# Seven-product attention gates, raw queries and keys beside the attention, and the attention's output projection beside the mLSTM heads

## The chip, the cores and the metric

The kernel runs on one core of a Trainium2 chip. The metric is the device time of one execution in microseconds (us). Before the change three executions took 2128.82, 2127.21 and 2130.36 us; their median is 2128.82 us. A further execution, run under the hardware profiler, took 2130.97 us, of which the program's own span, from its first to its last instruction, is 2129.0 us.

Engines are called by the names in the profile: PE is the matrix engine, PEld its loading of stationary operands, DVE, ACT and POOL the vector, scalar and general engines, SP the queue that issues most transfers.

## The reference, cut to what matters

One layer, 512 tokens, width 2048, everything in float32.

```python
h = rms_norm(x, norm_g)
proj = h @ w_in                       # split into the thirteen parts below
(q_a, k_a, v_a, o_a, i_a, f_a, z_a, c_q, c_kv, k_r, z_b, g_a, g_b) = split(proj)

qk_a = silu(causal_depthwise_conv(concat(q_a, k_a), conv_w))       # four taps
h_a = mlstm_chunkwise(q_a, k_a, v_a, i_a + bias, f_a + bias)       # 8 heads, 128 / 256 wide
h_a = rms_norm(h_a, mlstm_norm_g)
y_a = (sigmoid(o_a) * h_a * silu(z_a)) @ w_a

q_b = rms_norm(rms_norm(c_q) @ w_uq); k_b, v_b = from rms_norm(c_kv) @ w_ukv and k_r, with rope
o_b = causal_attention(q_b, k_b, v_b)                               # 16 heads
y_b = (o_b * silu(z_b)) @ w_b

out = x + (sigmoid(g_a) * y_a + sigmoid(g_b) * y_b) @ w_out
```

## The kernel before, in words

**Arithmetic.** PE multiplies float32 values that are split in two parts: `split` lets ACT copy the value to a rounded high part (line 105) and DVE subtract it to get the low part (line 106). `mm3` (lines 114 to 116) then issues three products, high by high, high by low, low by high. A product of 512 columns is the normal one: a 128x128 stationary block and 512 moving columns.

**Plain projections.** `proj_tok` produces rows of tokens: the stationary operand is a block of 128 tokens, the weights move. `proj_ch` produces rows of channels: the weights are stationary, 512 tokens move. Both are generators: after each 128 rows of the weights they yield the number of columns that they gave PE (6144 for a `proj_tok` of width 512, 4608 at width 384, 3072 for a `proj_ch` of two channel blocks). `load_w` fetches the weights through three small rings: raw, high and low.

**Stages, in program order.**

1. The latent projections and the normalisation of the input (0 to about 123 us).
2. `strassen`: five parts of the input projection (o_a, z_a, g_a, g_b, v_a), in ten jobs of 1024 columns. Each job makes a 2x2 block product with seven products instead of eight. A job has 28 steps of 12 products of 512 columns; the stationary operand is a combination of the token blocks, the combined weights move. `finish` hands the results to `tanh_out`, `silu_out` or `split_out`, which write them to DRAM.
3. Attention in eight pairs of heads. `pair_proj(p)` projects queries, keys and values of pair p from the latents; `pair_attn(p)` makes transposes, scores, softmax, transposed probabilities and values, in ten named steps, and stores the gated result to `gb_d[p]`. `pair_gate(p)` is the z_b gate of a pair: a plain `proj_ch` from the normalised input, 16 yields of 3072 columns (96 products), with a tanh and one DVE operation at the end; its result stays in the on-chip tile `gz`.
4. Queries and keys of the mLSTM: `block_qk(n)`, eight blocks of two heads each (queries and keys by turns), each a plain `proj_ch` of 96 products, with the convolution, the silu and the split after it on DVE and ACT (`conv_qk`). They read the normalised input, as the gates do.
5. Eight mLSTM heads. `head_load` fetches v, o and z; `head_mlstm` runs four steps of scores and four of values; `head_scale` and `head_out` finish a head, one head later, and store it to `ga_d[h]`.
6. `out_b(d)`: the attention's output projection with w_b, four column blocks of 16 yields of 6144 columns (12 products each). Its stationary operand comes from `gb_d` by way of `reload`, which fetches six blocks ahead into the pool `gp`.
7. The mLSTM's output projection with w_a, from `ga_d`, reloaded in the same way into the pool `g2p`, and the final projection with w_out (lines 1247 to 1276).

**What sets the order.** `weave(main, filler)` interleaves two generators: each number that the main one yields is a wish for filler columns, and the filler is advanced until at least that many have come; nothing is carried over to the next wish. The wishes are `KEYS_AHEAD` = 8000 once and `ATTN_STEP` = 7800 ten times for a pair, `MLSTM_STEP` = 6000 for each of a head's eight steps and `OUT_AHEAD` = 10000 four times after the last head. Under this, the framework's planner takes the program order as each engine's priority and moves later instructions up when earlier ones are not ready and their buffers are free.

Before the change the fillers are: in pairs 0 to 5 one gate and the next pair's projection each, in pair 6 the last projection, in pair 7 nothing; then blocks 0 to 2 run alone; block h+3 runs beside head h for h = 0 to 4; `out_b(0)` and `out_b(1)` run beside heads 5 to 7; `out_b(2)` and `out_b(3)` run alone after the heads.

**Memory.** Pools are opened and closed in program order, and a pool opened later may lie where a closed one was. The normalised input lies in `h8p` and `htp`; `gp` is opened where they were. The attention's tiles lie in `bpa` and `bpb`; the mLSTM's `bph` (17 slots) is opened there. `g2p` is opened where `bph` was. Short-lived tiles share the six slots of `tmp`. PSUM has five `acc` banks, used by projections, and three `aux` banks.

Of the kernel before, what the change touches and what calls it, by code (L numbers as in the profile page):

```python
# [19 lines left out]
P = 128  # L20
S = 512
# [18 lines left out]
KEYS_AHEAD, ATTN_STEP, MLSTM_STEP, OUT_AHEAD, G_AHEAD, CONV_WAIT = 8000, 7800, 6000, 10000, 6, 8  # L40
# [4 lines left out]
def hybrid_kernel(  # L45
# [396 lines left out]

    def split_out(dst):
        def done(t, src, inner):
            hi, lo = tmp(512, "oh", F32R), tmp(512, "ol", F32R)
            split(hi, lo, src)
            A.dma_start(dst[0][:, t, :], f32(hi))
            A.dma_start(dst[1][:, t, :], f32(lo))
        return done

    def strassen(jobs, comb):
# [45 lines left out]
        def mult(c, p, j):  # L497
# [52 lines left out]
        for src, col, outs in jobs:  # L550
            c = dict(src=src, col=col, outs=outs, x={}, ring={}, ps={})
            steps += [(c, p, j) for p in range(7) for j in range(H8 // 2)]
# [29 lines left out]
    jobs = []  # L582
    for off, dst, kind in ((OFF_OA, o_d, tanh_out), (OFF_ZA, z_d, silu_out), (OFF_GA, ga_g, tanh_out),
                           (OFF_GB, gb_g, tanh_out), (OFF_VA, v_d, split_out)):
        for i in range(2):
            jobs.append((w_in, off + 1024 * i, [kind(dst[2 * i]), kind(dst[2 * i + 1])]))
# [174 lines left out]
    def pair_proj(p, c):  # L761
        qn = big([P, T, 2, DN], F32, "qn")
# [144 lines left out]
    def pair_attn(p, c):  # L907
# [8 lines left out]
        for step in ("S00 S01", "X00 S02", "X01 S03", "X02 S10", "X03 S11", "O0 X10 S12", "X11 S13", "X12", "X13", "O1"):  # L916
            for w in step.split():
# [3 lines left out]
                elif w[0] == "X":  # L921
                    probs_t(c, u, int(w[2]))
                else:
                    drain(gates[p] or ())
                    values(p, c, u)
# [66 lines left out]

    cs = [dict() for _ in range(8)]
    first = pair_gate(0, cs[0])
    weave(chain(*lats), first)
    drain(first)
    drain(pair_proj(0, cs[0]))
    second = pair_gate(1, cs[1])
    weave(mlstm_gates(), second)
    drain(second)  # L1000
    gates = [None, None] + [pair_gate(p, cs[p]) for p in range(2, 8)]
# [10 lines left out]
    def conv_qk(p, base, blk, res, wait):  # L1012

        def evac(s, ps):
            k = blk + 2 * p + s
            xp = tmp(516, "xp")
            G.memset(xp[:, 0:3], 0.0)
            A.copy(xp[:, 3:515], ps)
            o = big([P, 2, S], F32R, "qkT")
            b = []  # L1020

            def taps(j0, j1):
                for j in range(j0, j1):
                    V.scalar_tensor_tensor(b[0], xp[:, j:j + S], cw[:, k, j:j + 1], b[0], ALU.mult, ALU.add)

            def first():
                b.extend((tmp(512, "cv"), tmp(512, "th")))
                with behind_weights():
                    V.tensor_scalar(b[0], xp[:, 3:515], cw[:, k, 3:4], None, ALU.mult)
                    taps(0, 1)  # L1030

            def second():
                taps(1, 3)
                A.activation(b[1], b[0], AF.Tanh, scale=0.5)

            def third():
                V.scalar_tensor_tensor(b[0], b[1], 1.0, b[0], ALU.add, ALU.mult)
                A.copy(o[:, 0, :], b[0])

            def fourth():  # L1040
                V.tensor_tensor(o[:, 1, :], b[0], f32(o[:, 0, :]), ALU.subtract)

            if s == 0:
                later.extend([lambda: None] * wait)
            later.extend((first, second, third, fourth))
            res.append(o)

        yield from proj_ch(load_h(base + p * 256), 2, get_n, KD, evac)
# [95 lines left out]
    def block_qk(n, wait=CONV_WAIT):  # L1144

        p, res = n // 2, []
        yield from conv_qk(p, *((OFF_KA, 8) if n % 2 else (OFF_QA, 0)), res, wait)
        for u in range(2):
            hs[2 * p + u]["kT" if n % 2 else "qT"] = res[u]
# [6 lines left out]
    def reload(src, pool, dst):  # L1156
        g = []

        def fetch():
            p, n = divmod(len(g), 2)  # L1160
            g.append(pool.tile([P, 2, S], F32R, tag="g", name=nm("g"), bufs=16))
            SP.dma_start(f32(g[-1][:, 1, :]), src[p][:, n, :])

        for _ in range(G_AHEAD):
            fetch()
        yield
        for k in range(KD):
            if len(g) < KD:
                fetch()
            split(g[k][:, 0, :], g[k][:, 1, :], f32(g[k][:, 1, :]))  # L1170
            dst.append((g[k][:, 0, :], g[k][:, 1, :]))
            yield

    def lazily(g, rest):
        def get(k):
            while k + 1 >= len(g) and len(g) < KD:
                next(rest)
            return g[k]
        return get

    u_t = []

    def out_b(d):
        u = up.tile([P, T, 512], F32, tag=f"u{d}", name=f"u{d}")
        SP.dma_start(u, gb_g[d])
        u_t.append(u)

        def evac(t, ps):
            V.scalar_tensor_tensor(u[:, t, :], u[:, t, :], 1.0, ps, ALU.add, ALU.mult)

        yield from proj_tok(load_w(w_b, d * 512, 512, KD), 512, get_gb, KD, evac)

    def heads():
        for h in range(H_A):
            ahead = head_load(h + 1, hs[h + 1]) if h + 1 < H_A else iter(())
            for n, want in enumerate(head_mlstm(h, hs[h])):
                next(ahead, None)
# [4 lines left out]
                yield want  # L1202
            drain(ahead)
            yield None
# [7 lines left out]
    filler = block_qk(3)  # L1212
    done = 0
    for want in heads():
        if want is not None:
            weave([want], filler)
            continue
        done += 1
        if done < 5:
            drain(filler)  # L1220
            filler = block_qk(done + 3, CONV_WAIT if done < 4 else 0)
        elif done == 5:
            drain(filler)
            close_pool("htp")
            close_pool("h8p")
            gp = open_pool("gp", "right")
            up = open_pool("up", "right")
            gB = []
            rest = reload(gb_d, gp, gB)
            next(rest)  # L1230
            get_gb = lazily(gB, rest)
            filler = chain(out_b(0), out_b(1))
    drain(filler)
# [85 lines left out]
```

## Time and profile before

| what | value |
|---|---|
| median of three executions | 2128.82 us |
| the profiled execution | 2130.97 us |
| its span | 2129.0 us |
| PE busy | 2100.9 us (99%), 10200 products |
| DVE, ACT, POOL busy | 1397.0 us (66%), 982.9 us (46%), 173.6 us (8%) |
| granted PE clock over the span | 0.999 |
| data moved | 292.31 MB, mean 137 GB/s |
| issues of 256 KB of w_in by `load_w` | 128, median 2.8 us to landing |
| issues of 512 KB of w_in by `strassen` | 160 (40 in `rx`, 120 in `rr`), 5.1 and 4.7 us to landing |

How to read it: "busy" of PE is the time in which at least one product is under way. Products are pipelined and overlap, so a product's own duration is longer than the time until the next one starts. A group of instructions is written as line, engine, operation, output <- inputs, form, count, then busy time and mean duration in ns. "SPq" and "ACTq" are the instruction queues that issue transfers.

### The profile page before, as it was taken

How to read it: one execution, taken by the hardware profiler on the slowest of the kernel's cores; microseconds unless marked ns; L12 is line 12 of the kernel's file. 1: busy time of each engine (PE TensorE's matmuls, PEld its weight loads, DVE VectorE, ACT ScalarE, POOL GpSimd, SP SyncE). 2: the span in 40 equal slices, each digit the busy share in tenths (PEclk: the TensorE clock that was granted, in tenths of full speed). 3: DMA queues.
4: the chain of work that ended last, by engine and by line, in shares of the span. 5: the costliest groups of instructions: out<-in, count | busy, mean ns of one | idle time of the engine just before them, and what ended most of it. 6: DMA issues, size and time to landing. Idle time of an engine off the chain costs nothing.

```text
span 2129.0 us, 28895 instructions
## 1 busy us (share of the span) xinstructions
PE 2100.9 (99%) x10200; PEld 1780.4 (84%) x10200; DVE 1397.0 (66%) x2260; ACT 982.9 (46%) x2025; POOL 173.6 (8%) x306
## 2 busy tenths in 40 slices
PE   8899999999999999999999999999999999999999
PEld 8888888888888888888888888788878788888889
DVE  6888878786786788746766666867785433443323
ACT  8544455444444444445555555545564322222221
POOL 0000010000000000022222222101111000000000
PEclk9999999999999999999999999999999999999999
DMA  6656437624633643832222222365564542332443
GB/s 163 167 184 188 142 108 236 207 91 129 197 102 102 192 148 101 263 88 79 80 80 81 82 77 75 123 199 162 164 209 134 183 138 96 121 123 91 138 130 118
DMA packets 208769, 292.31 MB, mean 137 GB/s; under 512 B 31600, under 2 KB 111856, under 8 KB 207600
## 3 DMA queue, kind: packets, MB, share of 16 engines
q1 hardware_dynamic: 192496, 263.20, 40.3%
q10 hardware_dynamic: 16128, 27.27, 3.6%
q8 instruction: 80, 1.31, 0.3%
q14 instruction: 65, 0.53, 0.1%
HBM read 244.27 MB, written 46.14 MB: 136 GB/s over the span
## 4 chain that ended last, share of the span: by engine, by line
PE 93%; DMA 2%; ACT 2%; DVE 1%; issue 1%; POOL 0%; SPq 0%; ACTq 0%; DVEq 0%; POOLq 0%
PE acc L115 16%; PE acc L116 16%; PE acc L114 16%; PE acc L518 8%; PE acc L519 8%; PE acc L517 8%; PE aux L519 4%; PE aux L518 4%; PE aux L517 4%; PE aux L114 2%; PE aux L116 2%; PE aux L115 2%; ACT junk L248 1%; PE aux L883 1%; PE aux L843 1%
## 5 line engine op out<-in xcount | busy, mean ns | idle before, releaser
L106 DVE TENSOR_TENSOR wlo<-raw,whi 128x512 fp32r<-128x512 f32 (+3 forms) x432 | 285.2, 663 | 390.5 <-PE acc L115 286.5
L105 ACT CAST whi<-raw 128x512 fp32r<-128x512 f32 (+3 forms) x432 | 259.1, 601 | 527.0 <-PE acc L116 356.5
L106 DVE TENSOR_TENSOR wl<-rx,wh 128x1024 fp32r<-128x1024 f32 x160 | 195.8, 1224 | 106.8 <-PE aux L518 57.3
L105 ACT CAST wh<-rx 128x1024 fp32r<-128x1024 f32 x160 | 168.8, 1055 | 172.8 <-PE acc L519 96.2
L115 PE MATMUL acc<-wlo,g 128*128 128x512 f32 x512 | 200.9, 392 | 3.6 <-DVE wlo L106 3.5
L114 PE MATMUL acc<-whi,g 128*128 128x512 f32 x512 | 200.1, 394 | 3.1 <-ACT whi L105 2.0
L105 ACT CAST wh<-rr 128x1024 fp32r<-128x1024 f32 x120 | 126.4, 1054 | 163.7 <-PE aux L519 91.7
L116 PE MATMUL acc<-whi,g 128*128 128x512 f32 x512 | 200.4, 392 | 1.1 <-DVE g L106 1.1
L106 DVE TENSOR_TENSOR wl<-rr,wh 128x1024 fp32r<-128x1024 f32 x120 | 146.3, 1219 | 25.3 <-PE aux L518 13.9
L518 PE MATMUL acc<-wl,sh 128*128 128x512 f32 x400 | 155.6, 389 | 0.0
L519 PE MATMUL acc<-wh,sl 128*128 128x512 f32 x400 | 155.6, 389 | 0.0
L517 PE MATMUL acc<-wh,sh 128*128 128x512 f32 x400 | 155.4, 389 | 0.0
L115 PEld LDWEIGHTS acc<-wlo,g 128*128 128x128 f32 x512 | 96.7, 189 | 25.1 <-DVE wlo L106 6.1
L116 PEld LDWEIGHTS acc<-whi,g 128*128 128x128 f32 x512 | 96.5, 189 | 21.7 <-DVE g L106 1.5
L114 PEld LDWEIGHTS acc<-whi,g 128*128 128x128 f32 x512 | 95.9, 188 | 22.3 <-ACT whi L105 2.2
L114 PE MATMUL acc<-whi,y 128*128 128x512 f32 (+1 forms) x320 | 111.1, 348 | 0.0
L116 PE MATMUL acc<-whi,y 128*128 128x512 f32 (+1 forms) x320 | 111.0, 347 | 0.0
L115 PE MATMUL acc<-wlo,y 128*128 128x512 f32 (+1 forms) x320 | 111.0, 347 | 0.0
L114 PE MATMUL acc<-h8h,whi 128*128 128x512 f32 x256 | 101.7, 397 | 0.0
L114 PE MATMUL acc<-ht,whi 128*128 128x512 f32 x256 | 101.6, 397 | 0.0
L116 PE MATMUL acc<-h8h,wlo 128*128 128x512 f32 x256 | 100.2, 391 | 0.1
L115 PE MATMUL acc<-h8l,whi 128*128 128x512 f32 x256 | 100.1, 391 | 0.0
(357 smaller groups left out, 5036.0 us busy)
## 6 DMA issues: line engine op xcount, KB each, us to landing
rr<-in_w_in SPq DMA_DIRECT2D x120, 512.0 KB, 4.7
raw<-in_w_in SPq DMA_DIRECT2D x128, 256.0 KB, 2.8
rx<-in_w_in SPq DMA_DIRECT2D x40, 512.0 KB, 5.1
raw<-in_w_b SPq DMA_DIRECT2D x64, 256.0 KB, 3.2
raw<-in_w_a SPq DMA_DIRECT2D x64, 256.0 KB, 3.0
raw<-in_w_out SPq DMA_DIRECT2D x64, 256.0 KB, 3.0
raw<-in_w_ukv SPq DMA_DIRECT2D x32, 256.0 KB, 2.9
raw<-in_w_uq SPq DMA_DIRECT2D x32, 192.0 KB, 2.4
```

The source lines that it names most:

```text
L105: hi = A.copy(dst_hi, src)
L106: lo = V.tensor_tensor(dst_lo, src, f32(dst_hi), ALU.subtract)
L114: PE.matmul(ps, lh, rh, start=start, stop=False)
L115: PE.matmul(ps, lh, rl, start=False, stop=False)
L116: PE.matmul(ps, ll, rh, start=False, stop=stop)
L248: A.activation(junk[:, :P], xr[:, t, :], AF.Square, accum_out=ssx[:, k, t:t + 1])
L517: PE.matmul(out[i], lh[:, tok], hi[:, n, :], start=first, stop=False, skip_group_check=cont)
L518: PE.matmul(out[i], lh[:, tok], lo[:, n, :], start=False, stop=False, skip_group_check=cont)
L519: PE.matmul(out[i], ll[:, tok], hi[:, n, :], start=False, stop=k == H8 - 1, skip_group_check=cont)
L843: PE.transpose(ps[:, t * P:(t + 1) * P], src(t), ident)
L883: PE.transpose(ps[:, j * P:(j + 1) * P], pr[:, j * P:(j + 1) * P], ident)
```

## The change

Four things are changed.

1. The z_b gate leaves the attention stage. It becomes two more jobs of `strassen`, ahead of v_a's. These jobs have a mark `ch`: the weights' combinations are stationary in blocks of 128 channels, and the combinations of the token blocks move, 256 columns at a time, so that a step has 24 products of 256 columns and the result stands in rows of channels. Two blocks of channels share one PSUM bank. `silu_out_ch` writes the gate to DRAM (`gz_d`), and `pair_proj` loads it into the tile `gz`. `pair_gate` is gone.
2. `block_qk(0)` to `(7)` take the gates' places: block 0 beside the latents' transposes, block 1 beside `mlstm_gates`, and blocks 2 to 7 as fillers of pairs 0 to 6, in the order "rest of a begun block, next pair's projection, further blocks". They store the raw queries and keys to DRAM (`qk_d`).
3. The convolution moves to the heads: `head_conv(h)` loads the raw rows of one head and runs the same operations one head ahead, in the same four parts, with the tanh written over the raw rows.
4. `out_b` becomes the only filler from pair 7 on: seven of its yields in pair 7, one with each of the six parts of `head_load(0)`, and the rest beside the heads. `gp` is opened, and the reload begun, before pair 7. `MLSTM_STEP` becomes 4500 and `OUT_AHEAD` 8000; `CONV_WAIT` is gone.

```diff
-KEYS_AHEAD, ATTN_STEP, MLSTM_STEP, OUT_AHEAD, G_AHEAD, CONV_WAIT = 8000, 7800, 6000, 10000, 6, 8
+KEYS_AHEAD, ATTN_STEP, MLSTM_STEP, OUT_AHEAD, G_AHEAD = 8000, 7800, 4500, 8000, 6
...
+    def silu_out_ch(dst):
+        def done(t, src, inner):
+            o = tmp(512, "ot")
+            A.activation(o, src, AF.Tanh, scale=0.5)
+            V.scalar_tensor_tensor(o, o, 1.0, src, ALU.add, ALU.mult)
+            n = (t // 2) * 256
+            A.dma_start(dst[t % 2][:, :, n:n + 256], o.rearrange("p (s c) -> p s c", s=2))
...
-                for i in range(2):
+                for i in range(4 if c["ch"] else 0):
+                    o, ch = out[i // 2][:, (i % 2) * 256:(i % 2 + 1) * 256], slice(i * P, (i + 1) * P)
+                    first = k == 0 and p not in (3, 5) and i % 2 == 0
+                    PE.matmul(o, hi[:, n, ch], lh, start=first, stop=False, skip_group_check=True)
+                    PE.matmul(o, hi[:, n, ch], ll, start=False, stop=False, skip_group_check=True)
+                    PE.matmul(o, lo[:, n, ch], lh, start=False, stop=k == H8 - 1, skip_group_check=True)
+                for i in range(0 if c["ch"] else 2):
...
     def pair_proj(p, c):
+        c["gz"] = big([P, 2, S], F32, "gz")
+        SP.dma_start(c["gz"], gz_d[p])
...
-    def pair_gate(p, c):
-        gz = c["gz"] = big([P, 2, S], F32, "gz")
+    def block_qk(n):
+        p, odd = divmod(n, 2)
         def evac(s, ps):
-            th = tmp(512, "th")
-            A.activation(th, ps, AF.Tanh, scale=0.5)
-            V.scalar_tensor_tensor(gz[:, s, :], th, 1.0, ps, ALU.add, ALU.mult)
-        yield from proj_ch(load_h(OFF_ZB + p * 256), 2, get_n, KD, evac)
+            x = tmp(512, "xq")
+            A.copy(x, ps)
+            A.dma_start(qk_d[2 * p + s][:, odd, :], x)
+        yield from proj_ch(load_h((OFF_KA if odd else OFF_QA) + p * 256), 2, get_n, KD, evac)
...
-    for p in range(8):
-        proj = pair_proj(p + 1, cs[p + 1]) if p < 7 else iter(())
-        weave(pair_attn(p, cs[p]), chain(gates[p] or (), proj, *gates[max(2, p + 1):p + 3]))
-        drain(proj)
+    for p in range(7):
+        proj = pair_proj(p + 1, cs[p + 1])
+        first = chain(ahead(True), proj)
+        weave(pair_attn(p, cs[p]), chain(first, ahead()))
+        drain(first)
         cs[p] = None
+    drain(ahead())
+    close_pool("htp")
+    close_pool("h8p")
+    gp = open_pool("gp", "right")
+    gB = []
+    rest = reload(gb_d, gp, gB)
+    next(rest)
+    get_gb = lazily(gB, rest)
+    filler = chain(*(out_b(d) for d in range(4)))
+    weave(pair_attn(7, cs[7]), islice(filler, 7))
...
+    def head_conv(h, c):
+        xs, parts = [], []
+        for n in range(2):
+            xp = tmp(516, "xp")
+            G.memset(xp[:, 0:3], 0.0)
+            SP.dma_start(xp[:, 3:515], qk_d[h][:, n, :])
+            xs.append(xp)
...
+        q, k = conv(0), conv(1)
+        for turn in ((), (), (), (q,), (q, k), (q, k), (q, k), (k,)):
+            for part in turn:
+                next(part)
+            yield
...
-    for n in range(3):
-        drain(block_qk(n, 0))
-    drain(head_load(0, hs[0]))
...
-    filler = block_qk(3)
...
-    drain(filler)
+    start = head_conv(0, hs[0])
+    for load in head_load(0, hs[0]):
+        next(start)
+        next(filler)
+    drain(start)
+    weave(heads(), filler)
     close_pool("bph")
     g2p = open_pool("g2p")
-    for d in range(2, 4):
-        drain(out_b(d))
+    drain(filler)
```

More of the change, by code (lines that the diff above doesn't have):

```diff
@@ L991, in mlstm_gates, with reload, fetch @@
                 V.tensor_tensor(ab[:, j, i, :], ab[:, j, i - 1, :], gs[:, i - 1, :], ALU.add)
+    def reload(src, pool, dst):
+        g = []
+        def fetch():
+            p, n = divmod(len(g), 2)
+            g.append(pool.tile([P, 2, S], F32R, tag="g", name=nm("g"), bufs=16))
+            SP.dma_start(f32(g[-1][:, 1, :]), src[p][:, n, :])
+        for _ in range(G_AHEAD):
+            fetch()
+        yield
+        for k in range(KD):
+            if len(g) < KD:
+                fetch()
+            split(g[k][:, 0, :], g[k][:, 1, :], f32(g[k][:, 1, :]))
+            dst.append((g[k][:, 0, :], g[k][:, 1, :]))
+            yield
@@ new lines, in lazily, with get, out_b, evac @@
+    def lazily(g, rest):
+        def get(k):
+            while k + 1 >= len(g) and len(g) < KD:
+                next(rest)
+            return g[k]
+        return get
+    u_t = []
+    def out_b(d):
+        def evac(t, ps):
+            u = u_t[d]
+            V.scalar_tensor_tensor(u[:, t, :], u[:, t, :], 1.0, ps, ALU.add, ALU.mult)
+        for k, want in enumerate(proj_tok(load_w(w_b, d * 512, 512, KD), 512, get_gb, KD, evac)):
+            if k == H8:
+                u_t.append(pools["up"][1].tile([P, T, 512], F32, tag=f"u{d}", name=f"u{d}"))
+                SP.dma_start(u_t[d], gb_g[d])
+            yield want
@@ L993, in hybrid_kernel @@
     cs = [dict() for _ in range(8)]
[L994 to L996 removed]
+    blocks = [block_qk(n) for n in range(8)]
+    weave(chain(*lats), blocks[0])
+    drain(blocks[0])
     drain(pair_proj(0, cs[0]))
[L998 to L1001, printed above, removed]
[L1002 to L1006 removed]
+    weave(mlstm_gates(), blocks[1])
@@ new lines, in hybrid_kernel, with ahead @@
+    drain(blocks[1])
+    del blocks[:2]
+    begun = []
+    def ahead(only_begun=False):
+        while blocks and (begun or not only_begun):
+            begun[:] = [True]
+            for want in blocks[0]:
+                yield want
+            del blocks[0], begun[:]
+    for p in range(7):
[3 more added lines that the diff above has]
+        drain(first)
+        cs[p] = None
+    drain(ahead())
@@ L1019, in evac @@
             o = big([P, 2, S], F32R, "qkT")
-            b = []
+            c["kT" if n else "qT"] = o
+            b = tmp(512, "cv")
             def taps(j0, j1):
                 for j in range(j0, j1):
[L1024 to L1045, printed above, removed]
@@ L1142, in head_out @@
         hs[h] = None
[L1144 to L1149, printed above, removed]
-    hs = [dict() for _ in range(H_A)]
-    for n in range(3):
-        drain(block_qk(n, 0))
-    drain(head_load(0, hs[0]))
[L1156 to L1191, printed above, removed]
+    hs = [dict() for _ in range(H_A)]
     def heads():
         for h in range(H_A):
-            ahead = head_load(h + 1, hs[h + 1]) if h + 1 < H_A else iter(())
+            conv = ahead = iter(())
+            if h + 1 < H_A:
+                conv, ahead = head_conv(h + 1, hs[h + 1]), head_load(h + 1, hs[h + 1])
             for n, want in enumerate(head_mlstm(h, hs[h])):
+                next(conv, None)
                 next(ahead, None)
```

62 lines of the change are left out of this document (29 added, 33 removed).

## The prediction

> **What bounds the kernel now.** I read the page's head, its slices and its chain first, then products by form and their starting times, then counts in windows.
>
> ```profile
> span 2129.0 us, 28895 instructions
> PE 2100.9 (99%) x10200; PEld 1780.4 (84%) x10200; DVE 1397.0 (66%) x2260; ACT 982.9 (46%) x2025; POOL 173.6 (8%) x306
> PEclk9999999999999999999999999999999999999999
> DMA  6656437624633643832222222365564542332443
> PE 93%; DMA 2%; ACT 2%; DVE 1%; issue 1%; POOL 0%; SPq 0%; ACTq 0%; DVEq 0%; POOLq 0%
> ```
>
> PE is busy for 99% of the span at the full granted clock, and 93% of the chain that ended last is PE. So the time is the number of products times their spacing, plus the stretches in which PE lacks work. The durations of products (about 390 and 280 ns) overlap; the spacing comes from starting times:
>
> ```profile
> 2079.11 0.28 PE L114 MATMUL acc<-whi,y 128*128 128x256 f32 x1
> ...
> 2125.06 0.28 PE L116 MATMUL acc<-whi,y 128*128 128x256 f32 x1
> L517 PE MATMUL acc<-wh,a x160: 388/389/397, 123.1 to 819.7; 128*128 128x512 f32 x160
> ...
> L519 PE MATMUL aux<-wh,h8l x160: 389/389/398, 189.8 to 885.4; 128*128 128x512 f32 x160
> ```
>
> The first pair of rows are the first and last of 384 products of 256 columns: 45.95 / 383 = 120.0 ns. The second pair bound the 3360 products of the seven-product stage: 762.3 / 3359 = 226.9 ns for 512 columns, with no pause. Half the columns thus cost 53% of the time. Where PE lacks work is seen by counting products on acc, then on aux:
>
> ```profile
> 1550.00:1600.00 50.00, 35.76 (x140) 0.97 0.65 218
> 1675.00:1725.00 50.00, 46.49 (x201) 1.00 0.70 232
> ...
> 1550.00:1600.00 50.00, 13.42 (x87) 0.97 0.65 218
> 1675.00:1725.00 50.00, 0.11 (x1) 1.00 0.70 232
> ```
>
> From 1550 to 1600 there are 140 products of 226.9 ns (31.8 us) and 87 of mostly 120 ns (10.4, with the longer score products about 11): some 7 us are lost, where the input's pool is exchanged for w_b's operand. From 1675 to 1725, 201 products are 45.6 us: 4.4 are lost, where the reload for w_a competes with w_b's weights.
>
> **Part a, the gates' products.** Removed: 8 gates x 96 = 768 products of 512 columns, 768 x 226.9 = 174.3 us. Added: 2 jobs x 28 steps x 24 = 1344 products of 256 columns, x 120.0 = 161.3 us. Net -13.0 us, all on the path. By eighths alone it would be 672 x 226.9 = 152.5 us; the narrow form gives 8.8 us of that back. The bounds are -13.0 and -21.8; I take -13.0, since the rows of 256 columns above are the same form on acc.
>
> The Trainium skill ("TensorE: Matmul & The Clock Gate", section "Back-to-back issue gap") gives a gap of N / 2.4 + 2.5 ns, 215.8 and 109.2 ns here; by it the sum would be 768 x 215.8 - 1344 x 109.2 = -19 us. The trace has 226.9 and 120.0, about 11 ns more for every product whatever its width, and the measurement decides.
>
> The steps' other work hides below products: 56 casts and subtractions of 1024 columns and 32 subtractions lie in a stage whose 3360 products above ran without a pause. The 16 stores of the gate, their 8 loads on SP, the 16 stores of raw rows on ACT's queue and 16 loads of them on SP are transfers of 256 to 512 KB in stages where the transfer engines are mostly 2 to 6 tenths busy (the DMA slices above). I cost them at nothing; without that cover, 24 loads of some 3 to 5 us stand in SP's order before w_in's and w_b's weights. The tanh, silu and convolution operations are the same in number.
>
> **Part b, the pool exchange.** The exchange at 1550 moves before pair 7, and the blocks that read the input are used up earlier still: a pair now wishes for three yields of a block ten times, less the projection's, about 21 a pair, so 96 yields end in pair 4. The reload then starts under attention products: the 7 us go. Late next: the start of the heads, where within six yields (16 us) come the loads of v, o, z (2 MB), raw rows, w_b's weights and w_b's operand splits. At the 218 GB/s of the row at 1550 the roughly 4.5 MB take 20 us. I give back 2: -5, between -7 and 0.
>
> **Part c, the last pairs.**
>
> ```profile
> 1239.87:1296.74 56.87, 56.83 (x303) 49.30 (x301) 38.93 (x95) 31.32 (x94) 14.87 (x18) 1.00 0.27 79
> 1296.74:1341.86 45.12, 42.30 (x237) 36.27 (x235) 33.60 (x87) 26.91 (x86) 14.38 (x18) 1.00 0.26 77
> ```
>
> The windows are pair 5, with gate and projection, and pair 6, with the projection and the first 30 products of block 0 that the planner moved up (303 - 237 = 66 fewer, of 96). Pair 6 should last 56.87 - 66 x 0.227 = 41.9 us and lasts 45.1: a pair without a block loses 3.2 us, as the softmax's chain on DVE and ACT shows through. Now the blocks are spent in pair 4, so pair 5 joins pair 6 in that state: products for 56.9 - 21.8 = 35.1 us under a chain that took 45.1. Pair 5 loses between 0 (if the next projection moves up) and 10; I take +5. Pair 7 gets seven yields (19 us) in place of block 0's: no change.
>
> **Part d, the end of the heads.** This decides the sign. out_b has 4 x 16 = 64 yields. Seven go to pair 7, six to `head_load(0)`. A wish of 4500 takes a whole yield of 6144, as 6000 did, so each of a head's eight steps takes one: 51 yields last through heads 0 to 5 and three steps of head 6. Thirteen steps, and all four wishes of `OUT_AHEAD`, find no filler. Before, out_b(2) and out_b(3) covered the close with 87 us of products.
>
> ```profile
> 1469.00:1497.60 28.60, 28.60 (x149) 24.51 (x148) 21.69 (x43) 16.65 (x42) 4.19 (x15) 1.00 0.54 166
> 1616.07:1644.67 28.60, 28.60 (x149) 24.50 (x148) 14.85 (x34) 13.60 (x36) 3.93 (x10) 1.00 0.27 93
> ```
>
> These are a head with a block and its convolutions, and a head with out_b. A head takes 28.6 us, of which the filler is 96 x 0.2269 = 21.8 and its own products 6.8. Own DVE work is 14.85 less eight splits of 0.69 (the row of L106 below) = 9.3, and the next head's convolution adds 21.69 - 14.85 = 6.8. For thirteen steps (1.6 heads): DVE 15.1, with the last convolution 21.9; PE 11. PE idles at least 4 us, at most 11 plus some 6 of latency; I take 7.
>
> After the last value product comes a chain with nothing beside it:
>
> ```profile
> 1649.46 0.28 PE L116 MATMUL aux<-vh,stb 128*128 128x258 f32 x1
> 1650.19 0.17 DVE L1116 SCALAR_TENSOR_TENSOR den<-num 128x4 f32<-128x4 f32 x1 [1.34 <-ACT num L1112]
> 1653.95 0.20 POOL L1125 TENSOR_TENSOR rsn<-rsn,den 128x4 f32<-128x4 f32 x1
> 1658.39 1.67 DVE L1132 SCALAR_TENSOR_TENSOR og<-num,rsn,og 128x256 f32<-128x256 f32 x4
> 1674.07 1.03 PE L1138 MATMUL aux<-ident,og 128*128 128x128 f32 x8
> 1676.45 0.47 SPq L1254 DMA_DIRECT2D gate<-gga  x1
> 1681.53 1.37 SPq L1162 DMA_DIRECT2D g<-ga  x3
> DMA to landing us min/median/max: 4.0/5.2/7.8
> 1686.41 1.29 ACT L105 CAST g<-g 128x512 fp32r<-128x512 f32 x2 [2.46 <-DMA g<-ga]
> 1687.06 0.69 DVE L106 TENSOR_TENSOR g<-g 128x512 fp32r<-128x512 f32 x1 [3.22 <-ACT g L105]
> ```
>
> From that product to the scale factors 1654.15 - 1649.46 = 4.7; scaling 1.7; transposes to the gate's load 1676.45 - 1674.07 = 2.4; its issue 0.5; the first block of w_a's operand 5.2 to land (the landing row is that of the reload's line); its split 0.62 + 0.69 = 1.3. Sum 15.8, less a microsecond of transposes: 14.8 us of empty PE. It cannot be shortened by earlier loads if a pool waits for the whole of the one before it, as here:
>
> ```profile
> L116 PE MATMUL acc<-h8h,wlo x256: 387/389/499, 886.5 to 1543.8; 128*128 128x512 f32 x128
> L116 PE MATMUL acc<-ht,wlo x256: 388/389/400, 900.7 to 1559.3; 128*128 128x512 f32 x128
> L1162 SPq DMA_DIRECT2D g<-gb x16: 319/430/611, 1556.8 to 1579.9; - x16
> L1162 SPq DMA_DIRECT2D g<-ga x16: 379/430/2725, 1681.5 to 1703.6; - x16
> ```
>
> Half of the input's tiles were last read at 1543.8, yet the first load into their place is issued at 1556.8, when the other half is almost done; and w_a's operand, most of it stored long before, is not fetched until head 7's transposes have run. Part d: +7 + 14.8 - 4.4 (the loss at 1675, gone) = +17.4, between 8 (4 + 8 for a chain with the operand already on its way) and 28.
>
> **Sum.** -13.0 - 5 + 5 + 17.4 = +4.4 us. The span becomes 2133.4, the profiled execution 2130.97 + 4.4 = 2135.4. That execution stands 2.15 us above the median of 2128.82, so I predict a median of 2133.2 us, 0.2% slower; 0.2% (4.3 us) is about what a measurement of this kernel tells from no change.
>
> **Rivals.** First, faster, by one mechanism: the end is covered. If `g2p` takes bph's slots one by one, head 0's to 5's rows (12 of 16 blocks) can be fetched and up to 12 x 2.72 = 32.6 us of w_a's products run during heads 6 and 7. It decides from the point at which the first load of `ga` is issued before head 7's last transposes. Then d is about 3 - 4.4, and the sum -13 - 5 + 5 - 1.4 = -14: 2114. For it: most of the 17 slots are idle by then. Against: the last four rows. Chance 0.15.
>
> Second, the cheap ends together with the same empty end: no loss in pair 5 and thirteen steps at DVE's pace: -13 - 7 + 0 + 14.4 = -6: 2123. For it: the planner moved 30 products up in pair 6. Chance 0.2.
>
> Third, the dear ends: pair 5 loses 10, the heads start 5 us late, and the thirteen steps run at the chain's latency: -13 + 0 + 10 + 24 = +21: 2150. For it: six slots of `tmp` now also hold raw rows until they are stored, and each convolution holds four. Chance 0.2. The empty end may also cost clock: the row at 1550 shows 0.97 granted where gaps stood, 1.5 us in 50. The Trainium skill, on the page named above (Part 1, "The HAM clock gate"), says the clock halves after an idle window of about 3.4 us and recovers after as long a busy one, which by it would add 1.7 us; no gap here is long enough to show it.
>
> My own case has 0.45, from 2128 to 2140. Of it 0.22 lie above +4.3 us and 0.23 within; of the second rival 0.13 is faster. Together: faster 0.28, same 0.30, slower 0.42. The range of 2116 to 2148 leaves out most of the first rival and the dearest end.
>
> **What would show it.** Part a: 1344 products of 256 columns with starts 120 ns apart, from some 735 to 895. Part b: no stretch of seven lost us at the reload of `gb`, its first load before pair 7. Part c: pair 5 short of products, with waits for `pr`. Part d: the last `out_b` product some 20 us before head 7's last values, then about 15 us of empty PE before the first product of w_a. I am wrong if w_a's products start before head 7's transposes, or if out_b still runs then.

## The result, and the profile after

The changed kernel takes 2156.54 us (median; 2155.99 to 2158.16), the kernel before 2128.39 in the same comparison: a ratio of 1.0133, 95% interval 1.0115 to 1.0150. It is 28 us slower, where 4 were forecast. The profiled execution has a span of 2154.3 us, 25.3 more than before.

The head and two slice rows of the page of the changed kernel:

```profile
span 2154.3 us, 30176 instructions
PE 2101.4 (98%) x10776; PEld 1803.1 (84%) x10776; DVE 1461.9 (68%) x2304; ACT 1007.7 (47%) x2025; POOL 167.4 (8%) x306
...
PE   8999999999999999999999999989999978999999
PEclk9999999999999999999999999999999988999999
```

Read against the page of before, PE's busy time is the same (2101.4 against 2100.9) while the span is 25 us longer, and PE's row has fallen in two places, the slice from 1400 to 1454 and the two from 1723 to 1831. The latter have lost clock too.

Busy time hides the change here, because durations of products overlap. So I counted products by form in each stretch, each at its own spacing (226.9 ns for 512 columns, 120 for 256 and 258, and so on), and took that from the stretch's length. What is left is PE's lost time:

| stretch, us of each trace | before | after | difference | step of the prediction |
|---|---|---|---|---|
| all products x spacing | 2081.5 | 2068.9 | -12.5 | a: -13.0 |
| lost, 0 to 125 (start) | 14.5 | 12.5 | -2.1 | none |
| lost, 125 to 875 (seven products) | about 0 | about 0 | 0 | a |
| lost, 875 to 1550 (pairs) | 12.7 | 27.0 | +14.3 | c: +5 |
| lost, 1550 to 1600 (before: the pool exchange; after: the heads' start) | 7.3 | 6.4 | -0.8 | b: -5 |
| lost, 1600 to 1800 (heads, close) | 4.9 | 31.5 | +26.6 | d: +17.4 |

The terms make +25.5, against 25.3 of span; behind 1800 both lose some 4 to 5 us. The start's 2 us are no more than it varies by: it differs by 3.8 us between two of the executions profiled for the experiments below, which do the same work there. The gates came out as forecast. These are the groups of the narrow products of the changed kernel (the numbers behind the line are the least, median and greatest ns, then the first and last start in us):

```profile
L527 PE MATMUL acc<-a,wh x64: 278/283/283, 730.4 to 822.2; 128*128 128x256 f32 x64
...
L529 PE MATMUL aux<-h8h,wl x64: 283/283/283, 799.7 to 891.5; 128*128 128x256 f32 x64
```

They bound the 1344 products: (891.5 - 730.4) / 1343 = 120.0 ns, with no pause.

The pairs are next. First the last three pairs and the one before them (window, length, busy us and count of PE, PEld, DVE, ACT and POOL, granted clock, DMA share, GB/s):

```profile
1371.90:1433.00 61.10, 54.43 (x287) 47.20 (x288) 40.46 (x100) 34.23 (x102) 14.58 (x18) 0.96 0.40 126
1433.00:1475.80 42.80, 40.55 (x222) 34.64 (x220) 34.09 (x88) 27.22 (x88) 14.17 (x18) 0.97 0.25 80
1475.80:1517.30 41.50, 36.91 (x200) 30.03 (x199) 32.37 (x85) 26.95 (x87) 14.38 (x18) 1.00 0.21 72
1517.30:1561.40 44.10, 43.95 (x224) 36.18 (x224) 30.32 (x77) 19.94 (x47) 2.23 (x11) 1.00 0.43 146
```

Then what PE waited for between 1425 and 1440 (total us, times, longest):

```profile
PE aux L867 <- POOL kn L829: 5.4, 1, 5.4
...
POOL rs_y L121 <- DVE ms L811: 11.4, 1, 11.4
```

And POOL's side of that wait in the timeline (start, us, operation):

```profile
1423.78 2.93 POOL L121 TENSOR_TENSOR rs_y<-ms,mhalf 128x16 f32<-128x16 f32 x1 [11.38 <-DVE ms L811]
...
1429.31 1.89 POOL L829 TENSOR_TENSOR kn<-kn,rs 128x1024 f32<-128x1024 f32 x1
```

Pair 4 (the first row) used up the last block, as forecast, yet it lasted 61.1 us and PE idles in it: at its end the transposes of projection 5 wait 5.4 us for POOL to scale `kn`. POOL itself had waited for the projection's mean squares (`ms`), and from there to the scaled `kn` it takes 1423.78 to 1431.20, 7.4 us, most of it with no product left for PE. The pairs that follow carry 222 and 200 products and last 42.8 and 41.5 us, bound by no engine. What PE waits for most in these two, from 1433 to 1517:

```profile
PE aux L907 <- DVE pr L894: 5.8, 4, 1.7
```

By the same count as in the table, pairs 4 to 7 lose some 9, 6, 7 and 1.5 us; before, pairs 5 to 7 lost some 1, 4 and 1.5. From 1400 to 1550 PE loses 22.8 us.

The close, in slices of ten us (same columns):

```profile
1740.00:1750.00 10.00, 10.00 (x51) 8.51 (x50) 8.30 (x17) 6.14 (x17) 2.17 (x11) 1.00 0.78 251
1750.00:1760.00 10.00, 4.71 (x37) 4.22 (x36) 10.00 (x22) 6.53 (x19) 0.00 (x0) 0.97 0.20 75
1760.00:1770.00 10.00, 5.41 (x16) 3.99 (x17) 6.60 (x18) 4.39 (x13) 3.51 (x10) 0.50 0.13 43
1770.00:1780.00 10.00, 5.81 (x36) 5.41 (x34) 1.59 (x8) 4.36 (x15) 2.07 (x7) 0.84 0.45 146
1780.00:1790.00 10.00, 2.58 (x10) 2.00 (x10) 2.33 (x6) 2.50 (x4) 0.00 (x0) 0.50 0.61 184
1790.00:1800.00 10.00, 10.00 (x38) 8.11 (x37) 9.12 (x16) 7.63 (x14) 0.00 (x0) 0.82 0.80 289
```

And its products in the timeline (start, us, operation; in brackets the idle time before it and its releaser):

```profile
1748.85 0.39 PE L116 MATMUL acc<-whi,g 128*128 128x512 f32 x1
...
1759.82 0.80 PE L114 MATMUL aux<-qkT,qkT 128*128 128x512 f32 x1 [3.93 <-ACT qkT L1122]
...
1775.54 0.28 PE L116 MATMUL aux<-vh,stb 128*128 128x258 f32 x1
...
1780.65 1.94 PE L1221 MATMUL aux<-ident,og 128*128 128x128 f32 x8 [4.84 <-DVE og L1215]
...
1789.36 0.79 PE L114 MATMUL acc<-whi,g 128*128 128x512 f32 x1 [6.77 <-ACT g L105]
1789.96 0.63 PE L115 MATMUL acc<-wlo,g 128*128 128x512 f32 x1
1790.38 0.63 PE L116 MATMUL acc<-whi,g 128*128 128x512 f32 x1
```

`out_b`'s last product is at 1748.85. In the next ten microseconds DVE is busy for all ten with the last convolution, the evacuations and scales, and PE for less than five. After that no engine is full: the head's own chain runs alone. Head 7's last value product starts at 1775.54, the first product of w_a 13.8 us later. From 1750 to 1800 stand 38 products on acc and 94 on aux: 8.6 + some 11.4 us of work, so 30 us are lost.

### The profile page after: what moved, and what is told of

The parts are those of the page before. It is cut to its first block, busy times and chain, and to the rows that moved or that the text cites. A ratio compares the mean times of both kernels' runs of the same rounds, so it can differ in the third digit from the quotient of the medians.

```text
span 2154.3 us, 30176 instructions
## 1 busy us (share of the span) xinstructions
PE 2101.4 (98%) x10776; PEld 1803.1 (84%) x10776; DVE 1461.9 (68%) x2304; ACT 1007.7 (47%) x2025; POOL 167.4 (8%) x306
## 5 line engine op out<-in xcount | busy, mean ns | idle before, releaser
L106 DVE TENSOR_TENSOR wlo<-raw,whi 128x512 fp32r<-128x512 f32 (+3 forms) x368 | 243.4, 663 | 327.1 <-PE acc L115 232.9
L105 ACT CAST whi<-raw 128x512 fp32r<-128x512 f32 (+3 forms) x368 | 218.9, 596 | 445.9 <-PE acc L116 322.7
L106 DVE TENSOR_TENSOR wl<-rx,wh 128x1024 fp32r<-128x1024 f32 x192 | 234.9, 1224 | 131.5 <-PE aux L535 58.8
L105 ACT CAST wh<-rx 128x1024 fp32r<-128x1024 f32 x192 | 202.4, 1055 | 211.3 <-PE acc L536 97.2
L105 ACT CAST wh<-rr 128x1024 fp32r<-128x1024 f32 x144 | 151.7, 1053 | 200.6 <-PE aux L536 91.7
L106 DVE TENSOR_TENSOR wl<-rr,wh 128x1024 fp32r<-128x1024 f32 x144 | 175.7, 1220 | 31.5 <-PE aux L535 13.9
L483 DVE TENSOR_TENSOR rx<-rr,rx 128x1024 f32<-128x1024 f32 x96 | 116.9, 1222 | 2.2
L114 PE MATMUL acc<-whi,lat 128*128 128x384 f32 (+1 forms) x256 | 94.9, 373 | 0.8 <-ACT junk L792 0.5
L115 PE MATMUL acc<-wlo,lat 128*128 128x384 f32 (+1 forms) x256 | 93.5, 365 | 0.0
L534 PE MATMUL aux<-wh,sh 128*128 128x512 f32 x240 | 93.4, 389 | 0.0
```

The source lines that it names most:

```text
L105: hi = A.copy(dst_hi, src)
L106: lo = V.tensor_tensor(dst_lo, src, f32(dst_hi), ALU.subtract)
L114: PE.matmul(ps, lh, rh, start=start, stop=False)
L115: PE.matmul(ps, lh, rl, start=False, stop=False)
L483: V.tensor_tensor(dst, a, b, ALU.subtract)
L534: PE.matmul(out[i], lh[:, tok], hi[:, n, :], start=first, stop=False, skip_group_check=cont)
```

## Experiments

My theory after the result: three losses that do not depend on each other. In the heads, a wish of 4500 that takes a whole yield of 6144 uses up `out_b` thirteen steps too early. In the pairs, the blocks are spent unevenly, and the rest of a begun block comes ahead of the projection. At the heads' start the moved loads and the first convolution collide. The rival ran: the close and the last pairs are bound by their own engines, and the filler's distribution changes little. Gains below are differences of the distance to the kernel before in the same comparison: the changed kernel stands at +28.2 us.

**Carrying the overshoot (heads).** A yield larger than the wish is now charged to the next wish.

```
-    weave(heads(), filler)
+    weave_carry(heads(), filler)
+    def weave_carry(main, filler):
+        owed = 0
+        for want in main:
+            owed += want
+            while owed > 0:
+                ...
+                owed -= got
```

> The changed kernel (2156.5 us), with one edit: beside the heads a yield's surplus is carried over to the next wish, so that 4500 columns a step are 4500 and not 6144. Theory A (out_b's yields run out in head 6, and the 30 us that PE lacks from 1750 to 1800 are that): the 51 yields now last through all eight heads (5.9 a head instead of 8) and five of them lie under the closing chain. What stays uncovered is the stretch from head 7's transposes to the first product of w_a, 8.7 us (1780.65 to 1789.36). Gain about 20 us: 2136. Rival B (the heads are bound by DVE and by the chain from score to value, not by the lack of products): a head doesn't get shorter than about 28 us, the end comes as late as before, gain under 5 us: over 2151.

2146.95 us, ratio 1.0094 (1.0073 to 1.0116): 7.5 us gained (10.3 by the spans). The windows and timeline of this kernel:

```profile
1750.00:1768.00 18.00, 18.00 (x96) 15.46 (x95) 8.19 (x19) 5.88 (x14) 2.23 (x6) 1.00 0.30 104
```

```profile
1767.70 1.03 PE L1231 MATMUL aux<-ident,og 128*128 128x128 f32 x8
1779.31 0.79 PE L114 MATMUL acc<-whi,g 128*128 128x512 f32 x1 [10.56 <-ACT g L105]
```

PE is full up to head 7's transposes, so the thirteen steps without filler are gone. What stays is the second half of the chain: from the transposes' last 10.6 us of empty PE until the first block of `ga` is loaded and split (ACT waits 8.9 us of it for that load). The gain fell short of the 20 us expected at two places: this rest is larger than the 8.7 us counted for it, and the heads from 1600 to 1750 now lose 7 us in place of 1.5. The filler now ends with the last head's steps, ahead of the closing chain.

**One block per pair, after the projection.**

```
-        first = chain(ahead(True), proj)
-        weave(pair_attn(p, cs[p]), chain(first, ahead()))
-        drain(first)
+        one = chain(proj, islice(ahead(), 16))
+        weave(pair_attn(p, cs[p]), one)
+        drain(one)
```

> The changed kernel with one edit: each of pairs 0 to 5 gets the next pair's projection first and then one block (16 yields), as the gates were given before, instead of 21 yields a pair until the blocks are spent in pair 4. Theory A (the blocks' bad spread costs the 21 us that PE lacks from 1400 to 1550, 6 of them because a begun block put the projection, and with it POOL's scaling of the keys, behind the end of pair 4): pairs 0 to 5 take 57 us each, only pairs 6 and 7 stay short. Gain 10 to 14 us: 2143 to 2147. Rival B (the sum of fillers is short by as much, wherever it is spread): the loss moves to pair 6 and the start of the heads, gain under 4 us: over 2152.

2140.40 us, 1.0063 (1.0042 to 1.0085): 14.1 us gained (15.7 by the spans), a little more than theory A gave. One pair, and the stretch that had lost 22.8 us, in windows of this kernel:

```profile
1174.10:1230.80 56.70, 56.70 (x302) 49.35 (x301) 37.79 (x93) 31.41 (x95) 14.89 (x18) 1.00 0.33 98
1400.00:1550.00 150.00, 146.25 (x771) 123.75 (x771) 111.65 (x273) 85.75 (x243) 31.45 (x47) 1.00 0.40 130
```

PE is busy throughout a pair with projection and one block. From 1400 to 1550 it now has 771 products in place of 722.

**Both together.**

> Both edits, the carry-over beside the heads and one block a pair. If the two losses are separate, the gains add: 2156.5 - 20 - 12 = 2124 or so, 2 to 6 us under the kernel before (2128.4). If they are one shortage that shows at two places, the second edit adds nothing to the larger one: 2136 or more.

2130.27 us, 1.0016 (1.0006 to 1.0026): 24.2 us gained, beside 7.5 + 14.1 = 21.6, so the gains add and the two losses are separate. It stays 6 us above the 2124 expected, which had counted 20 us for the carry-over. Nearly all of the 28 us lies in where the fillers stand.

**The gates in the form of 512 columns.** The jobs for the gates run in the form of the other seven-product jobs; their values then stand in the wrong places.

```
-            jobs.append((w_in, off + 1024 * i, [...], off == OFF_ZB))
+            jobs.append((w_in, off + 1024 * i, [...], False))
```

> The changed kernel with the gate's two seven-product jobs in the form of the other ten: 672 products of 512 columns instead of 1344 of 256. The gate's values come out in rows of tokens and are stored as if they were rows of channels, so they stand in the wrong places; all amounts of work after it are the same. Theory A (a product costs 11 ns beyond its columns, so the narrow form gives back 1344 x 120.0 - 672 x 226.9 = 8.8 us): 2147.7. Rival B (that part is hidden, or the jobs are bound by DVE's and ACT's combinations of the weights): 2155 to 2157.

2147.11 us, 1.0095 (1.0073 to 1.0117): 7.4 us gained. Products times spacing fall from 2068.9 to 2060.0, by 8.9. The gain agrees with that within the interval: the narrow form costs about what the spacing of 120.0 ns says. (The two spacings make 2 x 120.0 - 226.9 = 13.1 ns that a product costs beyond its columns, where the expectation has 11; the 8.8 us do not depend on it.)

**Smaller wishes of the heads.** On top of both: `MLSTM_STEP` 3900 in place of 4500.

> The kernel with both edits (2130.3 us), MLSTM_STEP 3900 instead of 4500: 41 yields beside the heads' steps and 5 under OUT_AHEAD, so that 5 (14 us) are left when bph closes. Theory A (the last 10.3 us without a product, between head 7's transposes and the first product of w_a, are the load and split of w_a's operand, and any 4 yields cover it): gain 8 to 10 us, 2120 to 2122. Rival B (the heads are already at DVE's pace: with both edits they take 23.6 us where their products need 22.7; a head with 5.1 yields has 20.6 us of products and 19.6 of DVE): they stay near 23.6, the five yields only move, and the time stays at 2128 to 2132.

2122.30 us, 0.9975 (0.9962 to 0.9987): faster than the kernel before by 4.2 us, 8.1 better than with 4500 (6.4 by the spans). From 1750 to 1800 the loss is now 1.3 us where both edits alone had left 12.2: filler is left over for the closing chain, and PE waits for no load there. The price is 8.3 us of small losses from 1600 to 1725 (4.1 in the kernel with both edits), and 10.2 at the heads' start (8.4).

**The block ahead of the projection.** The kernel with one block per pair, with that order alone reversed.

```
-        one = chain(proj, islice(ahead(), 16))
+        one = chain(islice(ahead(), 16), proj)
```

> The kernel with one block a pair (2140.4 us), with the order turned: the block before the next pair's projection. Theory A (a projection that ends late in a pair exposes POOL's rsqrt and scaling of the keys, the 5.6 us gap before pair 5 of the changed kernel): about that gap before each of pairs 1 to 6, 25 to 35 us in all, 2165 to 2175. Rival B (the gap came from the blocks' running out, not from the order): 2140 to 2143.

2195.29 us, 1.0316 (1.0295 to 1.0338): 68.8 above before, so 55 us lost by the order alone, more than I had expected. One pair in windows, and PE's greatest wait, of this kernel:

```profile
1184.40:1249.60 65.20, 60.01 (x302) 51.57 (x301) 37.90 (x92) 31.29 (x95) 13.67 (x18) 0.94 0.29 85
```

```profile
PE aux L867 <- POOL kn L829: 31.3, 6, 5.4
```

The pair with the same 302 products lasts 65.2 us in place of 56.7. Six times PE waits 5.2 to 5.4 us for the scaling of `kn` on POOL, the same wait and nearly the same length as the one at the end of pair 4 in the changed kernel. The waits are 31 of the 55 us. Behind each of them PE runs at half clock for 5 to 6 us, as in the first of these two windows, which begins where the first wait ends:

```profile
1182.70:1188.50 5.80, 5.80 (x22) 5.21 (x23) 2.23 (x4) 2.65 (x5) 1.63 (x3) 0.50 0.00 0
1188.50:1194.30 5.80, 5.80 (x33) 4.99 (x33) 5.23 (x12) 3.32 (x8) 1.11 (x3) 1.00 0.16 47
```

Products of 512 columns start 427 ns apart there in place of 227. By the count of products that costs 2.5 to 2.9 us each time, 16 us in all. Waits and clock make 47 of the 55 us; the other 8 are not traced.

**The gates' move alone.** The kernel before, with the gates by seven products and nothing in their place beside the attention.

> The kernel before (2126.3 us) with the first part of the change alone: the gates by seven products with weights stationary, loaded from DRAM; queries, keys and w_b stay where they were, and nothing takes the gates' place beside the attention. Theory A (12.5 us of products are saved, but the gates were the cover of the attention's chain): pairs 0 to 5 take 41 to 45 us for 35 us of products, 36 to 60 us lost, and some 10 more beside the latents' transposes and the mLSTM's gate values: 2160 to 2185. Rival B (the planner fills the pairs from what comes later): 2114 to 2125.

2156.88 us, 1.0136 (1.0114 to 1.0157): 30.4 above before, though its products need 12 us less, and 3 us under the range that theory A gave. Two pairs that have only a projection beside them:

```profile
1170.00:1210.80 40.80, 36.94 (x205) 31.04 (x204) 32.38 (x85) 25.23 (x85) 14.18 (x18) 1.00 0.23 72
1210.80:1251.70 40.90, 37.03 (x206) 31.03 (x205) 32.48 (x85) 25.33 (x85) 14.18 (x18) 1.00 0.22 72
```

And what PE waited for in these two:

```profile
PE aux L894 <- DVE pr L881: 6.8, 4, 2.1
```

Such a pair lasts 40.8 us for some 35 us of products: 5.9 are lost, mostly to the softmax's `pr`. So the gates' products had been cover: each pair that loses them and gets nothing else pays 6 us.

**Blocks spread evenly, but the begun block first.** The faster kernel (3900) with 14 yields of blocks in each pair, the rest of a begun block ahead of the projection.

> The kernel with the carry-over and MLSTM_STEP 3900, and the blocks spread evenly over seven pairs: 14 yields each, the rest of a begun block first, then the projection, then the next block. Theory A (a pair needs about 42 us of products: 15 of its own, 19 of projection, 8 and more of something else; pair 6 had nothing else): pair 6 loses its 4 us no more and nothing is lost elsewhere: 4 to 6 us less than with one block a pair, about 2116. Rival B (the rest of a begun block, up to 12 yields, delays the projection again): gaps before the pairs, 2120 to 2130.

2135.86 us, 1.0037 (1.0022 to 1.0051): 13.6 worse than with the projection first, as rival B had it but beyond its range. PE's greatest wait between 1400 and 1550 of this kernel:

```profile
PE aux L877 <- POOL kn L839: 8.6, 2, 5.4
```

So the even spread is worth less than the order. But a block ahead of the projection is not enough by itself: in the changed kernel's pair 1, too, the rest of a block (until 1198.7) stands ahead of the projection (1198.9 to 1224.4), and PE waits for `kn` only once in that whole kernel, at the end of pair 4. In pair 1 more block products follow the projection; in pair 4 nothing does. The wait shows where little or no filler is left behind the projection.

**Loads in another order at the heads' start.** The faster kernel with the loads of `u`, `v`, `o` and `z` put, on SP's queue, right behind the load on which w_b's filler waits.

```
-                SP.dma_start(u_t[d], gb_g[d])
+                with tc.issue_after(loads[0].ins):
+                    SP.dma_start(u_t[d], gb_g[d])
...
```

> The kernel with the carry-over, MLSTM_STEP 3900 and one block a pair (2122.3 us), with two kinds of loads tied behind the last load of weights in program order: the output gates u (1 MB each) and v, o, z of the next head (2 MB). Without the tie they run ahead of w_b's weights at the start of the heads, where 9.6 us are lost from 1550 to 1575 and the transfer engines are 100% busy (row 1560 to 1570). Theory A (these transfers in front of the weights are the loss): gain 3 to 6 us, 2116 to 2119. Rival B (DVE, 92 to 98% busy there with splits and head 0's convolution, is the loss): gain under 1.5 us, over 2120.8.

2120.32 us, 0.9967 (0.9954 to 0.9979), the fastest of the kernels here that do all the work: 2.1 us better than with 3900 alone, each against its own comparison. That lies between the two forecasts, and the intervals overlap (0.9962 to 0.9987 without the edit), so the time alone doesn't show a gain; the rows do. The heads' first 25 us in windows of this kernel:

```profile
1550.00:1575.00 25.00, 20.54 (x100) 15.58 (x99) 23.98 (x50) 16.15 (x46) 4.73 (x12) 1.00 0.55 189
```

The same stretch of the kernel without that edit:

```profile
1550.00:1575.00 25.00, 18.68 (x87) 14.65 (x87) 21.54 (x39) 14.18 (x38) 2.83 (x9) 0.93 0.84 293
```

The DMA share falls from 0.84 to 0.55 and the loss from 9.6 to 6.8 us. DVE now fills 24 of the 25 us. What this kernel still loses in the stages of the change is 7 us from 1450 to 1525, these 6.8, and 9.3 in the heads from 1600 to 1725.

**Head 0 without its convolution.** The kernel with 3900, with head 0's convolution and silu left out: it takes its raw rows.

> The same kernel (2122.3 us) without head 0's convolution and silu: its raw queries and keys are split directly, which takes 10 DVE operations (6.7 us) and two of ACT out of the start of the heads; head 0's values are those of the raw rows. Theory A (transfers): gain under 2 us, over 2120. Rival B (DVE): gain 4 to 7 us, 2115 to 2118.

2118.63 us, 0.9956 (0.9941 to 0.9971): 3.8 us better against its own comparison, just under what rival B named, again with intervals that overlap. The same stretch:

```profile
1550.00:1575.00 25.00, 22.51 (x112) 18.29 (x112) 22.91 (x46) 14.87 (x42) 3.30 (x10) 1.00 0.94 325
```

The loss falls from 9.6 to 3.8 us although the transfer engines are at 0.94. (The span is only 2.0 us shorter, since this execution lost 3.8 us more in its first 125 us.) In this kernel the first convolution is the larger part of what the heads' start loses, 5.8 us, and the order of the loads the smaller, 2.8.

**Wishes of 4200 in the fastest kernel.**

> As e9_in_place, with MLSTM_STEP 4200: 44 yields beside the heads' steps, 5 under OUT_AHEAD, 2 left for the end. If the heads lose by being at DVE's pace (8 us from 1600 to 1725 at 3900, 4 at 4500), 2 to 3 us come back there and up to 5 are lost at the end, where 5 us of products stand under a 10 us gap: 1 to 3 us slower than e9_in_place. If the heads are bound by the chain from score to value and not by DVE, the same as e9_in_place within 1 us.

2128.24 us, 1.0004 (0.9994 to 1.0013): 7.9 worse than with 3900 and the same loads, where 1 to 3 were expected. PE waits between 1740 and 1800:

```profile
PE acc L114 <- ACT g L105: 4.6, 1, 4.6
```

The closing chain is bare again (6.5 us lost from 1750 to 1775), while the heads lose no less than with 3900 (9.7 against 9.3 from 1600 to 1725). Yields spent too early are missing at the end, in the chain that has nothing else.

**Unread products at the close.** The changed kernel, with three products that nobody reads for each missing yield and 28 of them before w_a.

```
+    weave(heads(), chain(filler, warm()))
+    idle(28)
```

> The changed kernel (2156.5 us) with products that nobody reads, put where out_b's yields are missing: 3 of 512 columns (0.7 us) for each wish that finds no filler, and 28 (6.4 us) behind the last head, in front of w_a's; they need no DVE, ACT or transfer. The work for the result is the same. Theory A (beside the empty time itself, the end pays for a lower clock: from 1755 to 1794 the granted clock is 0.54 to 0.67, and the first ten products of w_a are 427 ns apart instead of 227): these ten alone give 2.0 us, the thirty score and value products at 320 to 430 ns up to 3 more: 2152 to 2154.5. Rival B (the chain on DVE, ACT and POOL and w_a's operand set the end, whatever the clock): within 1 us of 2156.5, or slower by the products that get in the way, up to 4 us.

2153.35 us, 1.0131 (1.0114 to 1.0148). Against its own comparison it stands at +27.6, 0.5 us below the changed kernel, and by the spans 2.4: the time alone does not tell it from no change. The trace does, in the rows of the last chain:

```profile
1755.00:1776.00 21.00, 19.41 (x112) 16.23 (x111) 13.30 (x34) 12.66 (x38) 3.59 (x10) 1.00 0.21 75
1776.00:1789.00 13.00, 11.48 (x46) 8.86 (x45) 2.71 (x8) 2.51 (x4) 1.99 (x6) 0.87 0.68 215
1789.00:1794.00 5.00, 5.00 (x23) 4.11 (x23) 4.01 (x7) 3.69 (x8) 0.00 (x0) 1.00 1.03 383
```

The changed kernel's own rows for the same three windows:

```profile
1755.00:1776.00 21.00, 12.30 (x57) 10.15 (x55) 12.18 (x30) 11.44 (x34) 3.59 (x10) 0.67 0.16 59
1776.00:1789.00 13.00, 1.94 (x8) 1.51 (x8) 2.68 (x10) 2.17 (x6) 1.99 (x6) 0.65 0.69 211
1789.00:1794.00 5.00, 4.64 (x12) 3.64 (x13) 4.04 (x6) 4.02 (x7) 0.00 (x0) 0.54 1.01 370
```

With PE kept busy the clock stays granted, and w_a's first products start 227 ns apart in place of 427. But the first one starts at 1789.29, as before at 1789.36: the chain to it runs for the most part on other engines and a load, and a PE at full clock doesn't shorten it. In w_a's first products the clock is about 2 of the 30 us lost there, and the whole kernel gains no more than 2.4 by the spans; the rest is lack of work.

## Why the prediction was wrong

The time of 2156.5 lies above the range. Three steps failed: in part d the price of the thirteen steps without filler (7 us forecast, some 15 measured), in part c the pair that uses up the blocks, taken as covered (some 8 us that weren't in the sum), and in part b the heads' start (2 us forecast, 6.4 measured).

- **Part a, -13.0: right.** The products fell by 12.5 us, and the narrow form costs the forecast 8.8 (8.9 by the products of the experiment without it). Rows of 256 columns from another stage gave the price of the new form to a tenth of a nanosecond. The formula that the prediction quotes beside it, from the section "Back-to-back issue gap" of the Trainium skill's page "TensorE: Matmul & The Clock Gate", stands there for a single, isolated product, and this is a stream; the measured spacing decided, so no term rests on it.
- **Part b, -5: the move was right, the gain didn't stay (-0.8).** The reload of `gb` is issued from 1388.4 us on in place of 1556.8, before pair 7 as forecast, and its 7 us are gone. I gave back 2 for the heads' start; it lost 6.4. I priced the transfers alone, by GB/s, and counted the moved convolutions as "the same in number" and so as free. In the kernel with 3900 the first convolution is the larger share of what the heads' start loses (5.8 of 9.6 us, and 2.8 for the order of the loads). For the changed kernel itself this is not shown: there DVE is busy for 18.3 and 17.9 us of the two stretches of 25 from 1550 to 1600, the transfer engines are at 0.97 and 0.71, and how the 6.4 us divide stays open.
- **Part c, +5: +14.3.** The loss of a pair without a block was sized well: pair 5 lost some 5 us more than before, and a pair of the run of the gates' move alone loses 5.9, both with the waits for `pr` that I named. The failed step is "the blocks are spent in pair 4, so pair 5 joins pair 6": it lets only pair 5 pay. Pair 4 lost most, some 8 us more than a covered pair: `first = chain(ahead(True), proj)` puts the last of the blocks ahead of projection 5, nothing is left behind it, and POOL's `kn` comes 5.4 us late. The run with the block first shows that wait six times at 5.2 to 5.4 us, the evenly spread one twice, at 3.2 and 5.4. Pair 6, whose products fell from 237 to 200, lost some 2 us more than before; pair 7 came out as forecast.
- **Part d, +17.4: +26.6, the mechanism right.** `out_b` ended in head 6, as counted from whole yields, and the chain to w_a was bare. The chain measured 13.8 us from the last value product to w_a's first, 12.8 without a microsecond of transposes, where I had 14.8. The thirteen steps were the mis-sized term: I took 7 from "PE idles at least 4 us, at most 11 plus some 6 of latency"; 30.0 - 12.8 - 2.0 of clock leaves some 15, near the upper bound. The lower value assumed that DVE's work and PE's overlap. In the rows they don't: DVE is full while PE waits from 1750 to 1760, then both are half idle.
- **The clock** was named with the third rival, on the argument that a bare end might cost it. Now the rows show 0.50 granted from 1760 to 1770 and from 1780 to 1790, behind gaps of 3.9 to 6.8 us, and ten products 427 ns apart, 2.0 us more than at full spacing. The Trainium skill ("TensorE: Matmul & The Clock Gate", Part 1, "The HAM clock gate") says that the clock halves after an idle window of about 3.4 us and comes back after as long a busy one. The close agrees with it: the prediction's estimate of 1.7 us, worked out from that page, stands near the 2.0 measured, and w_a's products come to full spacing 4.3 us after the first. But the changed kernel also has 0.93 granted from 1575 to 1600, where no wait of PE is longer than 0.7 us.
- **The rivals.** The first (covered end) fell by the trace: w_a's first load is issued at 1784, after head 7's transposes. The second (cheap ends) fell by the pairs and by the thirteen steps. The third, the dear ends, is the one that happened, with c and d each still past its price. I gave it 0.2 and stopped the range at 2148, short of its own 2150.

All three errors have one sign. Each time I took the middle of a bound or less for what happens when cover goes or work collides, and each time PE's loss came out near or above the upper end. The fewer products do pay once the fillers are placed otherwise: the fastest kernel above takes 2120.3 us, 0.9967 of the kernel before.

## What to carry to other kernels

When products move out of a stage, first ask what they covered: here 12.5 us of products were saved and the time rose by 28, nearly all of which came back by spreading the same filler otherwise. Count filler in the units in which it is really handed out, against every step that wishes for it, and keep some for the closing chain, where nothing else is left; wishes of 4500 met with units of 6144 spend a third too much. Put the filler whose result has a long way through other engines (the projection, with POOL's scaling behind it) ahead of the one that has none, so that something is left to run while that way is gone.

## What was not expected of the hardware

- POOL's scaling of `kn` sets a wait of nearly constant length, 5.2 to 5.4 us, where no filler is left behind the projection. With the projection first and one block behind it, in the kernel with 3900, it is in none of PE's waits.
- What the half clock costs depends on what stands behind the wait. In the close it was some 2 us of 30, most of which passed with no product to run. With the block first, PE had products enough behind each wait of `kn`, and the clock made 16 of 55 us.
- Busy transfer engines alone did not decide the loss: from 1550 to 1575 the kernel without head 0's convolution lost 3.8 us with the transfer engines at 0.94 and DVE busy for 22.9 us, the one with the loads in another order 6.8 us with 0.55 and DVE busy for 24.0.
